# Four more outputs of three norms from x * g, an earlier memory norm, two heads' Gram products in turns, and shared blocks for decay and rate, in a two-block kernel on one core

## The chip, the cores and the metric

The kernel runs on one core of one Trainium2 chip. A core has TensorE (PE, matmuls), VectorE (DVE), ScalarE (ACT), GpSimd (POOL) and SyncE (SP), which here issues DMAs, and each engine executes its own instructions in order. The metric is the device time of one execution in microseconds (us); lower is better.

## The reference

Two transformer-like blocks follow each other on 256 positions of width 1024. The first has three branches (window attention, spatial gating, pooling), gated and merged, then attention to a memory, then a squared-ReLU network. The second prepends 16 meta positions (so 272), has an RWKV-7 layer and a stick-breaking attention layer, each with a convolutional gated network. Nearly each part begins with an RMS norm. What the change touches is this:

```python
def rmsnorm(x, g):
    y = xf * lax.rsqrt(jnp.mean(xf * xf, axis=-1, keepdims=True) + EPS)
    return y * g
# first block
h = rmsnorm(x, g_norm[l, 0])
q, k, v, su, sv, pc, gate = split_columns(h @ w_in[l])
ya = window_sink_attention(q, k, v, attn_sinks[l])
...
merged = jnp.sum(gates * proj, axis=2)        # proj: ya, yb, yc times w_branch
mem_n = rmsnorm(mem, g_mem[l])
...
yf = jnp.square(jax.nn.relu(hf @ w_up[l])) @ w_down[l]
# second block, RWKV-7
w_log = -jax.nn.softplus(-(w0 + jnp.tanh(xw @ w1) @ w2)) - 0.5
a = jax.nn.sigmoid(a0 + (xa @ a1) @ a2)
def step(S, inp):
    sa = jnp.einsum('bhij,bhj->bhi', S, a_t)
    S = S * w_t + sa[..., None] * b_t + v_t[..., None] * k_t
    return S, jnp.einsum('bhij,bhj->bhi', S, r_t)
```

The kernel computes the recurrence in chunks of 64 positions; the Gram products are the products of the chunk's keys with its keys and receptances, of which each head (64 wide, so two heads share 128 partitions) has its own.

## The kernel before, in words

Activations lie transposed, with the features on the partitions: a tensor is 8 tiles (`kc`) of 128 features by 256 (or 272, or 258 in the last layer) positions. Weights come as blocks of 128 x 128 in the order in which the program reads them, eight blocks (512 KB) to a DMA on SP; class `Weights` (L118) issues these DMAs ahead. ACT rounds a group to `whi` and DVE (or POOL, in some stages) subtracts to get `wlo`, and a block is then three matmuls in `mm3` (L382): `wh` by `xh` (L388), `wh` by `xl` (L389) and `wl` by `xh` (L390), where `xh`, `xl` are the two halves of the activation. A "whole" group (`W.whole`, L347 for those of the diff) lands straight in a `whi` or `wlo` buffer, is not split, and a block is one full-precision matmul (L385), which the trace records as two.

`dense` (L403) computes one output of 128 features: all `kc` in a row into one bank, then an eviction. Banks of `pd` are the ordinary ones; `sc` banks (pool `pss`) serve small work.

Class `Norm` (L456 on) normalizes. `steps` writes `raw` = x * g (split, or whole in full precision) and sums the squares. `first` (L490) computes the first four outputs from `raw` by `outer` (L515, `kc` in the outer loop, four banks), since these do not need the root mean square; the result is multiplied by rstd on DVE at the eviction (`ev`). Meanwhile `split` makes the normalized operand: DVE `nt` (x * g * rstd), ACT `xh`, DVE `xl`. The second four outputs (`then`) come by `outer` from it, and the remaining ones by `dense`. `then` is given in four places: w_in, w_up (whole first four), the first network's up-projection of the second block (f_up0, 272 positions, whole first four), and that of the last layer (f_up1, 258 positions, split).

In the first block the gate products (24 outputs of w_in) run with side work between them (`together` of attention, gating and pooling, three steps after each product). Then 24 branch products follow, for features 0 to 3 and then 4 to 7, in each group the gating and pooling branch (n = 1, 2) first and the attention branch (n = 0) after; `norm_mem` (L722), the memory's norm, is the side work there.

In the RWKV stage `decay` (L1091 on) has 16 products with one block each, decay and rate in turns (each weight has 64 rows, padded with zero rows to 128), into the two `pd` banks; ACT takes each with a sigmoid into `LA`. Later the recurrence runs as generators under a planner with due times; its dense products fill the gaps, and Tile's scheduler writes the final order of each engine. `gram(b)` makes for each of two pairs of heads `jj` and head `hh` one product `p0` and four products `pm` in two `f` banks, and evacuates them: ACT copies to `B`, DVE masks into `AK` and `RS`. `fmm` is a matmul (its line in the trace is L986, a helper). All ACT, DVE and POOL work has L214, the line of a helper that records it.

Of the kernel before, what the change touches and what calls it, by code (L numbers as in the profile page):

```python
# [18 lines left out]
P = 128  # L19
D = 1024  # L20
KC = 8
# [27 lines left out]
WHOLE = [n // BLK_G for n in (624, 1456)]  # L49
N_BLOCKS = (42 * 8 + 24 * 4 + 64 + 64 + 32 + 32 + 256 + 256) + (256 + 16 + 16 + 32 + 2 * (352 + 176)) + 256  # L50
# [221 lines left out]
def drain(side):  # L272
    for _ in side:
        pass
# [14 lines left out]
def model(ctx: ExitStack, tc: tile.TileContext, a: dict, out: bass.AP, stage=None):  # L289
# [56 lines left out]
    for first in WHOLE:  # L346
        W.whole.update(range(first, first + 4))  # L347
# [108 lines left out]
    class Norm:  # L456
# [33 lines left out]
        def first(self, items, then=(), ahead=None):  # L490
            def rstd():
                self.r = rstd_of(self.sums, self.n)

            assert not self.whole or len(W.order) // BLK_G in WHOLE
            tiles = outer([x[:2] for x in items], self.raw, self.n, 2, ahead, rstd)
            W.hold = []
            nc.stop()
            dst = xpair(self.n) if then else None
            for i, ((_, ft, ev), ps) in enumerate(zip(items, tiles)):
                if then:  # L500
                    self.split(dst, range(4 * i, 4 * i + 4) if i < 2 else ())
                    if i == 0:
                        table["hold"] += casts
                t = ep[0].tile([P, T], F32, tag="ev", name="ev")[:, :self.n]
                vtt(t, ps, self.r, op=ALU.mult)
                ev(ft, t)
            if then:
                for (_, ft, ev), ps in zip(then, outer([x[:2] for x in then], dst, self.n, 1)):
                    ev(ft, ps)
            return dst  # L510
# [31 lines left out]
    with tc.tile_pool(name="b1", bufs=1) as b1, tc.tile_pool(name="b2", bufs=2) as b2:  # L542
# [172 lines left out]
        side = together(attention(), gating(), pooling())  # L715
        interleave(jobs, side, 3)
        drain(side)

        merged = xpair(S)
        memn = xpair(S)  # L720

        def norm_mem():  # L722
            acc = new_acc(S)
            for kc in range(KC):
                sumsq(mem[:, kc, :], acc, kc == 0, S)
            yield
            r = rstd_of([acc], S)
            for kc in range(KC):
                norm_split(lambda kc: mem[:, kc, :], "g_mem", 0, S, r, memn, (kc,))
                yield  # L730

# [15 lines left out]
        side = norm_mem()  # L747
        order = [(n, ft) for fts in (range(NBR), range(NBR, 8)) for ns in ((1, 2), (0,)) for ft in fts for n in ns]
        interleave([dense(f"w_br{n}", ft, 4, (ya, yb, yc)[n], S, ev_merge(n)) for n, ft in order], side)
        drain(side)  # L750
# [125 lines left out]
    with tc.tile_pool(name="f1", bufs=1) as f1:  # L876
# [30 lines left out]
        W.whole.update(range(group, group + 40))  # L907
# [70 lines left out]
    def rwkv():  # L978
# [11 lines left out]
        with tc.tile_pool(name="rp", bufs=1) as rp, ExitStack() as es:  # L990
# [99 lines left out]

            def decay(n):  # L1091
# [5 lines left out]
            lora = iter(range(16))  # L1097
            decay(16)
# [42 lines left out]

            def scp(tag, shape):
                tag = MAP.get(tag, tag)
                return pq.tile(shape, F32, tag=tag, name=tag, bufs=NBANK[tag])
# [68 lines left out]
            def gram(b):  # L1213
# [20 lines left out]
                for jj in range(2):  # L1234
# [9 lines left out]
                    strict, incl = (lambda q, n, i=i: amask[q, 64 * i:64 * i + 64].unsqueeze(1).broadcast_to([q.stop - q.start, n, 64]) for i in range(2))  # L1244
                    for hh in range(2):
                        r, o = half[hh], other[hh]
                        p0, pm = scp("f", [P, 2, 64]), scp("f", [P, 4, 2, 64])
                        fmm(p0, lhsT=bk2(BK, r, 0), rhs=KR[b][r, jj, :, 0:64], start=True, stop=True)
                        for c in range(4):
                            cs = slice(64 * c + 64, 64 * c + 128)  # L1250
                            im = fmm(pm[:, c], lhsT=bk2(BK, r, c + 1), rhs=KR[b][r, jj, :, cs], start=True, stop=True)
                        nc.scalar.copy(B[r, 8 + jj, :], p0[r, 0, :])
                        vtt(AK[o, jj, 0, :], p0[o, 0, :], amask[o, 0:64], op=ALU.mult)
                        vtt(RS[:, jj, 0, hh, :], p0[:, 1, :], amask[:, 64:128], op=ALU.mult)
                        nc.scalar.copy(B[r, 4 * jj:4 * jj + 4, :], pm[r, :, 0, :])
                        vtt(AK[o, jj, 1:5, :], pm[o, :, 0, :], strict(o, 4), op=ALU.mult)
                        vtt(RS[:, jj, 1:5, hh, :], pm[:, :, 1, :], incl(al, 4), op=ALU.mult)
                        yield 1.1, 1.5
# [513 lines left out]
def arrays(i):  # L1772
# [24 lines left out]
    for n in range(3):  # L1797
# [6 lines left out]
        rw_w2=_pad(i["rw_w2_2"][0], rows=P), rw_a2=_pad(i["rw_a2_2"][0], rows=P, at=(64, 0)), rw_g2=_pad(i["rw_g2_2"][0], rows=2 * P),  # L1804
# [35 lines left out]
```

## Time and profile before

| | us |
|---|---|
| median of 3 runs | 1325.83 (1320.94 to 1328.16) |
| the profiled execution | 1322.63 |
| its span in the trace | 1320.9 |
| TensorE busy | 1268.0 (96%) |
| VectorE busy | 894.8 (68%) |
| ScalarE busy | 705.6 (53%) |
| GpSimd busy | 178.5 (14%) |
| mean granted TensorE clock | 0.988 |

The span is from the first to the last instruction of the profiled execution. An engine's busy time divided by the span is its share. The chain that ended last follows the end of the program back from each instruction to what released it, so it tells whose work sets the end; the groups of instructions and waits tell how long one instruction takes and what an engine waited for.

### The profile page before, as it was taken

To read this page: it belongs to the slowest core of one execution; us is meant where nothing else is said; L and a number is where in the kernel's file an instruction comes from. 1 tells how busy PE (TensorE), PEld (TensorE's weight loads), DVE (VectorE), ACT (ScalarE), POOL (GpSimd) and SP (SyncE) were. 2 spreads that over 40 slices of the span, in tenths; PEclk is the share of its full clock that TensorE was granted. 3 is DMA by queue.
4 is the path that set the end of the run, shared out by engine and by line. 5 is a ranking of instruction groups with operands and counts; after the bars stand their busy time and mean duration, and the time that the engine had idled before them with its cause. 6 is when DMAs were issued, how large, how long until landed. Compare 5 with 4: busy or idle time off the path is not lost.

```text
span 1320.9 us, 25715 instructions
## 1 busy us (share of the span) xinstructions
PE 1268.0 (96%) x10188; PEld 1176.1 (89%) x10188; DVE 894.8 (68%) x1812; ACT 705.6 (53%) x1349; POOL 178.5 (14%) x237
## 2 busy tenths in 40 slices
PE   5999998999999989999999999999999999899997
PEld 5999998888999976877877679999999989899997
DVE  6576586857664457567486468786567557989954
ACT  6566555675554434433242256665457666666643
POOL 1000000000000000434211002553000000135500
PEclk9999999998999999999999989999999999999999
DMA  7554455433555653432202125555554333655663
GB/s 257 157 175 134 155 149 162 153 128 128 178 190 179 188 192 120 128 96 65 71 13 64 50 65 166 170 176 178 175 170 142 125 95 87 191 171 178 191 182 106
DMA packets 54984, 188.16 MB, mean 142 GB/s; under 512 B 7598, under 2 KB 9792, under 8 KB 54736
## 3 DMA queue, kind: packets, MB, share of 16 engines
q1 hardware_dynamic: 53856, 185.27, 44.6%
q8 instruction: 80, 1.31, 0.4%
q0 software_dynamic: 464, 0.73, 0.3%
q10 hardware_dynamic: 544, 0.52, 0.1%
q14 instruction: 40, 0.33, 0.1%
HBM read 185.56 MB, written 1.05 MB: 141 GB/s over the span
## 4 chain that ended last, share of the span: by engine, by line
PE 84%; DVE 10%; ACT 3%; DMA 1%; issue 1%; POOL 1%; SPq 0%; DVEq 0%; ACTq 0%; POOLq 0%
PE pd L388 19%; PE pd L390 19%; PE pd L389 19%; PE pd L385 9%; PE l L986 3%; PE f L986 2%; DVE wlo L214 2%; PE sc L389 1%; PE sc L390 1%; PE sc L385 1%; DVE sh L214 1%; PE sc L388 1%; PE s L986 1%; DVE nt L214 1%; PE sc L1608 1%
## 5 line engine op out<-in xcount | busy, mean ns | idle before, releaser
L214 DVE TENSOR_TENSOR wlo<-raw,whi 128x1024 fp32r<-128x1024 f32 x270 | 332.5, 1233 | 208.6 <-ACT whi L214 204.1
L214 ACT CAST whi<-raw 128x1024 fp32r<-128x1024 f32 x298 | 312.2, 1049 | 299.4 <-PE pd L389 201.4
L388 PE MATMUL pd<-xh,whi 128*128 128x256 f32 (+2 forms) x1264 | 364.0, 289 | 18.9 <-ACT xh L214 12.4
L389 PE MATMUL pd<-xl,whi 128*128 128x256 f32 (+2 forms) x1264 | 361.2, 286 | 6.3 <-DVE xl L214 6.3
L390 PE MATMUL pd<-xh,wlo 128*128 128x256 f32 (+2 forms) x1264 | 361.0, 287 | 0.7 <-DVE wlo L214 0.6
L388 PEld LDWEIGHTS pd<-xh,whi 128*128 128x128 f32 x1264 | 241.8, 192 | 22.8 <-ACT xh L214 13.8
L389 PEld LDWEIGHTS pd<-xl,whi 128*128 128x128 f32 x1264 | 242.6, 192 | 7.4 <-DVE xl L214 7.2
L390 PEld LDWEIGHTS pd<-xh,wlo 128*128 128x128 f32 x1264 | 242.2, 192 | 1.6 <-DVE wlo L214 1.2
L389 PE MATMUL pd<-gl,whi 128*128 128x272 f32 (+1 forms) x352 | 100.1, 285 | 0.0
L388 PE MATMUL pd<-gh,whi 128*128 128x272 f32 (+1 forms) x352 | 100.0, 285 | 0.0
L390 PE MATMUL pd<-gh,wlo 128*128 128x272 f32 (+1 forms) x352 | 99.9, 284 | 0.0
L214 DVE SCALAR_TENSOR_TENSOR c<-pd,vec,c 128x256 f32<-128x256 f32 (+3 forms) x148 | 72.0, 487 | 13.6 <-ACT c L214 11.9
L214 POOL TENSOR_TENSOR wlo<-raw,whi 128x1024 fp32r<-128x1024 f32 x28 | 67.2, 2401 | 77.4 <-ACT whi L214 77.4
L390 PE MATMUL pd<-uh,wlo 128*128 128x256 f32 x256 | 72.5, 283 | 0.4 <-DVE wlo L214 0.4
L388 PE MATMUL pd<-uh,whi 128*128 128x256 f32 x256 | 72.6, 284 | 0.0
L389 PE MATMUL pd<-ul,whi 128*128 128x256 f32 x256 | 72.4, 283 | 0.0
L214 POOL TENSOR_TENSOR s<-s,c 128x272 f32<-128x272 f32 (+1 forms) x44 | 41.9, 953 | 191.3 <-ACT s L214 191.3
L390 PEld LDWEIGHTS pd<-gh,wlo 128*128 128x128 f32 x352 | 66.3, 188 | 0.0
L389 PEld LDWEIGHTS pd<-gl,whi 128*128 128x128 f32 x352 | 66.3, 188 | 0.0
L388 PEld LDWEIGHTS pd<-gh,whi 128*128 128x128 f32 x352 | 66.2, 188 | 0.0
L214 POOL MEMSET hn<- 128x8 f32 x1 | 0.1, 147 | 479.5 <-PE sc L436 479.5
L214 DVE TENSOR_TENSOR gl<-c,gh 128x272 fp32r<-128x272 f32 (+1 forms) x44 | 56.4, 1284 | 1.1 <-ACT gh L214 1.1
(443 smaller groups left out, 2650.8 us busy)
## 6 DMA issues: line engine op xcount, KB each, us to landing
raw<-in_wblk SPq DMA_DIRECT2D x298, 512.0 KB, 3.6
whi<-in_wblk SPq DMA_DIRECT2D x24, 512.0 KB, 3.5
wlo<-in_wblk SPq DMA_DIRECT2D x24, 512.0 KB, 3.6
mem<-in_memT SPq DMA_DIRECT2D x1, 1024.0 KB, 6.7
h<-in_xT SPq DMA_DIRECT2D x4, 128.0 KB, 5.5
h<-in_xT POOLq DMA_DIRECT2D x4, 128.0 KB, 6.5
out<-h SPq DMA_DIRECT2D x2, 256.0 KB, 2.4
out<-h ACTq DMA_DIRECT2D x2, 256.0 KB, 2.5
```

Of the source, the lines that this page charges most:

```text
L214: ins = f(*args, **kw)
L385: first = mm(ps, lhsT=wh, rhs=xh, start=start, stop=stop)
L388: first = mm(ps, lhsT=wh, rhs=xh, start=start, stop=False)
L389: mm(ps, lhsT=wh, rhs=xl, start=False, stop=False)
L390: W.used(mm(ps, lhsT=wl, rhs=xh, start=False, stop=stop))
L986: latest[:] = [nc.tensor.matmul(*args, **kw)]
L1608: mm(z[hh][:, c0:c0 + n], lhsT=k[j][r, s0:s0 + 128], rhs=q[j][r, q0 - Q0:], start=False, stop=True, skip_group_check=True)
```

## The change

1. `first` computes the second four outputs by `dense` from `raw`, the operand of the first four, and multiplies each by rstd at its eviction. The outputs 5 and 8 go to `pd` banks, 6 and 7 to `sc` banks. The normalized operand is still made, for output nine and on. In w_up and f_up0 the second four's weights become whole: the two places have eight whole groups each instead of four.
2. `norm_mem` becomes side work of the gate products, after gating; the branch products have none.
3. In `gram` the `p0` of both heads come first, are evacuated, and then the `pm` of both heads are issued in turns and evacuated.
4. The weights of decay and rate share a block (upper 64 rows the one, lower 64 the other), so 8 blocks instead of 16. Each product uses half the rows, one into a `pd` bank, the other into an `f` bank.

```diff
-WHOLE = [n // BLK_G for n in (624, 1456)]
-N_BLOCKS = (...) + (256 + 16 + 16 + 32 + 2 * (352 + 176)) + 256
+WHOLE = [n // BLK_G for n in (624, 1448)]
+N_BLOCKS = (...) + (256 + 16 + 8 + 32 + 2 * (352 + 176)) + 256
...
-        W.whole.update(range(first, first + 4))
+        W.whole.update(range(first, first + 8))
...
+            def scaled(ft, ev, ps):
+                t = ep[0].tile([P, T], F32, tag="ev", name="ev")[:, :self.n]
+                vtt(t, ps, self.r, op=ALU.mult)
+                ev(ft, t)
...
-            if then:
-                for (_, ft, ev), ps in zip(then, outer([x[:2] for x in then], dst, self.n, 1)):
-                    ev(ft, ps)
+                scaled(ft, ev, ps)
+            old = bank["dense"]
+            for i, (name, ft, ev) in enumerate(then):
+                if i in (1, 2):
+                    bank["dense"] = lambda: pss.tile([P, 512], F32, tag="sc", name="sc")
+                dense(name, ft, KC, self.raw, self.n, lambda ft, ps: scaled(ft, ev, ps))()
+                bank["dense"] = old
...
-        side = together(attention(), gating(), pooling())
+        side = together(attention(), both(gating(), norm_mem()), pooling())
...
-        side = norm_mem()
-        interleave([dense(f"w_br{n}", ft, 4, (ya, yb, yc)[n], S, ev_merge(n)) for n, ft in order], side)
-        drain(side)
+        for n, ft in order:
+            dense(f"w_br{n}", ft, 4, (ya, yb, yc)[n], S, ev_merge(n))()
...
             def decay(n):
                 for _ in range(n):
-                    j, i = divmod(next(lora), 2)
-                    nm, bias = (("rw_w2", "w0"), ("rw_a2", "a0"))[i]
-                    dense(nm, j, 1, hwa, T, lambda ft, ps: act(LA[:, ft, i, :], ps, AF.Sigmoid, bias=vcol(bias, ft)))()
-            decay(16)
+                    j = next(lora)
+                    w = W.blocks([("rw_wa2", 0, j)])[0]
+                    for i, (r, ps) in enumerate(zip(half, (bank["dense"]()[:, :T], scp("f", [P, T])))):
+                        ins = mm(ps, lhsT=w[r, :], rhs=t[r], start=True, stop=True)
+                        act(LA[:, j, i, :], ps, AF.Sigmoid, bias=vcol(("w0", "a0")[i], j))
+                    W.used(ins)
+            decay(8)
...
+                    p0 = [scp("f", [P, 2, 64]) for _ in half]
+                    for hh, r in enumerate(half):
+                        fmm(p0[hh], lhsT=bk2(BK, r, 0), rhs=KR[b][r, jj, :, 0:64], start=True, stop=True)
                     for hh in range(2):
...
-                        p0, pm = scp("f", [P, 2, 64]), scp("f", [P, 4, 2, 64])
-                        fmm(p0, lhsT=bk2(BK, r, 0), rhs=KR[b][r, jj, :, 0:64], start=True, stop=True)
-                        for c in range(4):
-                            im = fmm(pm[:, c], lhsT=bk2(BK, r, c + 1), rhs=KR[b][r, jj, :, cs], start=True, stop=True)
...
-                        yield 1.1, 1.5
+                    yield 0.3, 1.0
+                    pm = [scp("f", [P, 4, 2, 64]) for _ in half]
+                    for c in range(4):
+                        for hh, r in enumerate(half):
+                            im = fmm(pm[hh][:, c], lhsT=bk2(BK, r, c + 1), rhs=KR[b][r, jj, :, cs], start=True, stop=True)
...
+                    yield 0.9, 2.0
```

How the order of the instructions changes, at the places of which the prediction speaks, follows from the compiled programs. The first is PE after the first four outputs of w_in (`xh_120`, `xl_121` are the halves of x * g, `xh_311`, `xl_312` those of the normalized operand). Before:

```order
L388 MATMUL sc_145<-xh_120,whi_257 128x256
L389 MATMUL sc_145<-xl_121,whi_257 128x256
L390 MATMUL sc_145<-xh_120,wlo_258 128x256
L388 MATMUL pd_357<-xh_311,whi_363 128x256
L388 MATMUL sc_358<-xh_311,whi_363 128x256
L388 MATMUL sc_359<-xh_311,whi_363 128x256
L388 MATMUL sc_360<-xh_311,whi_363 128x256
L389 MATMUL pd_357<-xl_312,whi_363 128x256
L390 MATMUL pd_357<-xh_311,wlo_364 128x256
```

Now:

```order
L388 MATMUL sc_145<-xh_120,whi_257 128x256
L389 MATMUL sc_145<-xl_121,whi_257 128x256
L390 MATMUL sc_145<-xh_120,wlo_258 128x256
L388 MATMUL pd_357<-xh_120,whi_360 128x256
L389 MATMUL pd_357<-xl_121,whi_360 128x256
L390 MATMUL pd_357<-xh_120,wlo_361 128x256
L388 MATMUL pd_357<-xh_120,whi_360 128x256
L389 MATMUL pd_357<-xl_121,whi_360 128x256
```

The four outputs no longer stand side by side for each `kc`; one output runs through, from the operand that is already there, and `xh_311` first appears 96 matmuls later.

The second place is PE in the RWKV stage, at the Gram products of the second of eight pairs of heads (L986 before, L993 now, `f<-KR,BK`; L385 are dense products). Before, one head's five and then the other's:

```order
L986 MATMUL f_6141<-KR_5697,BK_6026 128x128
...
L986 MATMUL f_6142<-KR_5697,BK_6026 128x128 x4
L986 MATMUL f_6184<-KR_5697,BK_6026 128x128
L385 MATMUL pd_6101<-xh_5921,wlo_6018 128x272 x7
L385 MATMUL pd_6137<-xh_5921,whi_6040 128x272 x5
L986 MATMUL f_6185<-KR_5697,BK_6026 128x128 x4
```

Now, in that pair, which alone comes out in turns (first part), and in the third, as in the other six (second part):

```order
L993 MATMUL f_6174<-KR_5635,BK_6026 128x128
...
L993 MATMUL f_6175<-KR_5635,BK_6026 128x128
...
L993 MATMUL f_6211<-KR_5635,BK_6026 128x128
L993 MATMUL f_6212<-KR_5635,BK_6026 128x128
L993 MATMUL f_6211<-KR_5635,BK_6026 128x128
L993 MATMUL f_6212<-KR_5635,BK_6026 128x128
...
L993 MATMUL f_6251<-KR_5636,BK_6120 128x128
L993 MATMUL f_6252<-KR_5636,BK_6120 128x128
...
L993 MATMUL f_6297<-KR_5636,BK_6120 128x128 x4
L993 MATMUL f_6298<-KR_5636,BK_6120 128x128 x4
```

The two `p0` stand before all `pm`, both `f` banks go to them together, and the four `pm` of a head still stand together except in the first of these pairs.

The third place is PE at the last attention head in the first block (`sc<-kT,qT` its scores, `sc<-ident,p` its transposes, `sc<-pT,vtok` its output). Before, the scores stand among the products with `ybh`, `ych`, long before the transposes. Now:

```order
L626 MATMUL sc_2014<-kT_136,qT_135 128x128
L626 MATMUL sc_2015<-kT_136,qT_135 128x128
L388 MATMUL pd_2349<-yah_833,whi_2294 128x256
...
L390 MATMUL pd_2366<-yah_833,wlo_2330 128x256
L646 MATMUL sc_2034<-ident_93,p_2027 128x128 x2
L653 MATMUL sc_2039<-pT_2037,vtok_839 64x128 x2
L388 MATMUL pd_2326<-yah_833,whi_2294 128x256
```

Between the scores and the transposes stand 21 matmuls of the first products that read the attention's result.

## Rows read from the trace of the kernel before

**Rows 1.** The page: an engine's busy time and share; the chain's shares by engine.

```profile
PE 1268.0 (96%) x10188; PEld 1176.1 (89%) x10188; DVE 894.8 (68%) x1812; ACT 705.6 (53%) x1349; POOL 178.5 (14%) x237
...
PE 84%; DVE 10%; ACT 3%; DMA 1%; issue 1%; POOL 1%; SPq 0%; DVEq 0%; ACTq 0%; POOLq 0%
```

**Rows 2.** Windows: stretch, length, PE busy (instructions), clock, DMA share, GB/s; w_in, w_up, f_up0.

```profile
25.42:45.20 19.78, 14.40 (x99) 0.83 0.44 134
...
303.40:321.55 18.15, 15.11 (x100) 0.81 0.27 88
781.70:800.20 18.50, 15.36 (x99) 0.82 0.25 81
```

**Rows 3.** Waits of PE by line and releaser: us in total, times, longest.

```profile
PE pd L388 <- ACT xh L214: 12.4, 5, 5.9
```

**Rows 4.** A window inside w_in's second four, same columns as rows 2.

```profile
30.00:37.10 7.10, 5.41 (x25) 0.52 0.22 74
```

**Rows 5.** Timeline of PE: start, length, instruction; a split product, then a whole one.

```profile
219.43 0.28 PE L388 MATMUL pd<-xh,whi 128*128 128x256 f32 x1
...
220.39 0.28 PE L390 MATMUL pd<-xh,wlo 128*128 128x256 f32 x1
...
289.98 1.03 PE L385 MATMUL sc<-xg,whi 128*128 128x256 f32 x4
290.85 1.03 PE L385 MATMUL pd<-xg,whi 128*128 128x256 f32 x4
```

**Rows 6.** Timeline of DVE after rstd in w_in.

```profile
26.84 1.67 DVE L214 SCALAR_TENSOR_TENSOR nt<-h,vec,rstd 128x256 f32<-128x256 f32 x4
28.42 0.75 DVE L214 TENSOR_TENSOR ev<-pd,rstd 128x256 f32<-128x256 f32 x2
...
30.08 1.22 DVE L214 TENSOR_TENSOR wlo<-raw,whi 128x1024 fp32r<-128x1024 f32 x1
31.21 1.09 DVE L214 TENSOR_TENSOR xl<-nt,xh 128x256 fp32r<-128x256 f32 x3
```

**Rows 7.** A window in f_up1's second four, same columns as rows 2.

```profile
1148.90:1152.60 3.70, 0.14 (x2) 1.00 0.44 142
```

**Rows 8.** Branch products: window (PE, PEld, DVE, ACT, POOL busy, clock, DMA), timeline of DVE and PE.

```profile
189.00:208.00 19.00, 15.55 (x121) 14.36 (x120) 18.50 (x44) 10.48 (x22) 0.00 (x0) 1.00 0.40 132
...
190.07 1.67 DVE L214 SCALAR_TENSOR_TENSOR nt<-mem,vec,rstd 128x256 f32<-128x256 f32 x4
...
176.21 0.49 PE L619 MATMUL sc<-kT,qT 64*128 64x128 f32 x4
...
188.49 0.29 DVE L214 TENSOR_TENSOR yal<-sc,yah 128x128 fp32r<-128x128 f32 x1 [1.84 <-ACT yah L214]
```

**Rows 9.** Timeline of PE and ACT at the products of decay and rate (in brackets: idle before).

```profile
523.69 5.10 PE L385 MATMUL pd<-wa,wlo 128*128 128x272 f32 x16
...
527.06 0.95 ACT L214 ACTIVATE LA<-pd,vec 128x272 f32<-128x272 f32 x2 [0.35 <-PE pd L385]
528.36 0.95 ACT L214 ACTIVATE LA<-pd,vec 128x272 f32<-128x272 f32 x2 [0.35 <-PE pd L385]
```

**Rows 10.** Timeline: Gram products, chunk products with halves in turns, a hand-over of an `f` bank.

```profile
557.19 1.16 PE L986 MATMUL f<-KR,BK 64*128 64x128 f32 x10
558.28 0.50 PE L385 MATMUL pd<-xh,wlo 128*128 128x272 f32 x1
...
642.38 0.45 PE L986 MATMUL l<-room 128*64 128x64 f32 x8
642.77 0.45 PE L986 MATMUL l<-KR,S 64*64 64x64 f32 x8
643.05 0.28 PE L986 MATMUL l<-xkh,xkl 64*64 64x64 f32 x4
...
553.37 0.49 PE L986 MATMUL f<-KR,BK 64*128 64x128 f32 x2
...
556.05 0.47 DVE L214 TENSOR_TENSOR room<-f,amask 64x64 f32<-64x64 f32 x2
```

More of the change, by code (lines that the diff above doesn't have):

```diff
@@ L48 @@
 WARM1 = 10
-WHOLE = [n // BLK_G for n in (624, 1456)]
-N_BLOCKS = (42 * 8 + 24 * 4 + 64 + 64 + 32 + 32 + 256 + 256) + (256 + 16 + 16 + 32 + 2 * (352 + 176)) + 256
+WHOLE = [n // BLK_G for n in (624, 1448)]
+N_BLOCKS = (42 * 8 + 24 * 4 + 64 + 64 + 32 + 32 + 256 + 256) + (256 + 16 + 8 + 32 + 2 * (352 + 176)) + 256
 N_DMA = -(-N_BLOCKS // BLK_G)
@@ L503, in first @@
                         table["hold"] += casts
-                t = ep[0].tile([P, T], F32, tag="ev", name="ev")[:, :self.n]
-                vtt(t, ps, self.r, op=ALU.mult)
-                ev(ft, t)
-            if then:
-                for (_, ft, ev), ps in zip(then, outer([x[:2] for x in then], dst, self.n, 1)):
-                    ev(ft, ps)
+                scaled(ft, ev, ps)
[5 more added lines that the diff above has]
+                bank["dense"] = old
             return dst
@@ L714, in model @@
         jobs = [dense("w_in", 18 + i, KC, h0, S, ev_in) for i in range(24)]
-        side = together(attention(), gating(), pooling())
-        interleave(jobs, side, 3)
-        drain(side)
-        merged = xpair(S)
         memn = xpair(S)
@@ L730, in norm_mem @@
                 yield
+        side = together(attention(), both(gating(), norm_mem()), pooling())
+        interleave(jobs, side, 3)
+        drain(side)
+        merged = xpair(S)
         mg = {}
@@ L745, in ev_merge @@
             return ev
-        side = norm_mem()
         order = [(n, ft) for fts in (range(NBR), range(NBR, 8)) for ns in ((1, 2), (0,)) for ft in fts for n in ns]
-        interleave([dense(f"w_br{n}", ft, 4, (ya, yb, yc)[n], S, ev_merge(n)) for n, ft in order], side)
-        drain(side)
+        for n, ft in order:
+            dense(f"w_br{n}", ft, 4, (ya, yb, yc)[n], S, ev_merge(n))()
     def add_post(post, steps, width, stop, pool=(), ready=1, fill=0):
@@ L906, in model @@
         group = len(W.order) // BLK_G + 32
-        W.whole.update(range(group, group + 40))
+        W.whole.update(range(group, group + 39))
         W.first[group] = scale_wa(False)
@@ L1089, in rwkv, with scp @@
             act(t[0:64], t[0:64], AF.Tanh)
+            def scp(tag, shape):
+                tag = MAP.get(tag, tag)
+                return pq.tile(shape, F32, tag=tag, name=tag, bufs=NBANK[tag])
             def decay(n):
                 for _ in range(n):
-                    j, i = divmod(next(lora), 2)
-                    nm, bias = (("rw_w2", "w0"), ("rw_a2", "a0"))[i]
-                    dense(nm, j, 1, hwa, T, lambda ft, ps: act(LA[:, ft, i, :], ps, AF.Sigmoid, bias=vcol(bias, ft)))()
-            lora = iter(range(16))
-            decay(16)
+                    j = next(lora)
[4 more added lines that the diff above has]
+                    W.used(ins)
+            lora = iter(range(8))
+            decay(8)
             base = tc.cur_priority
@@ L1140, in ev_v @@
                 xdone[2] = i0
-            def scp(tag, shape):
-                tag = MAP.get(tag, tag)
-                return pq.tile(shape, F32, tag=tag, name=tag, bufs=NBANK[tag])
             def wt(tag):
@@ L1255, in gram @@
-                        nc.scalar.copy(B[r, 4 * jj:4 * jj + 4, :], pm[r, :, 0, :])
-                        vtt(AK[o, jj, 1:5, :], pm[o, :, 0, :], strict(o, 4), op=ALU.mult)
-                        vtt(RS[:, jj, 1:5, hh, :], pm[:, :, 1, :], incl(al, 4), op=ALU.mult)
-                        yield 1.1, 1.5
+                        nc.scalar.copy(B[r, 8 + jj, :], p0[hh][r, 0, :])
+                        vtt(AK[o, jj, 0, :], p0[hh][o, 0, :], amask[o, 0:64], op=ALU.mult)
+                        vtt(RS[:, jj, 0, hh, :], p0[hh][:, 1, :], amask[:, 64:128], op=ALU.mult)
@@ new lines, in gram @@
+                    yield 0.3, 1.0
+                    pm = [scp("f", [P, 4, 2, 64]) for _ in half]
+                    for c in range(4):
+                        cs = slice(64 * c + 64, 64 * c + 128)
+                        for hh, r in enumerate(half):
+                            im = fmm(pm[hh][:, c], lhsT=bk2(BK, r, c + 1), rhs=KR[b][r, jj, :, cs], start=True, stop=True)
+                    for hh in range(2):
+                        r, o = half[hh], other[hh]
+                        nc.scalar.copy(B[r, 4 * jj:4 * jj + 4, :], pm[hh][r, :, 0, :])
+                        vtt(AK[o, jj, 1:5, :], pm[hh][o, :, 0, :], strict(o, 4), op=ALU.mult)
+                        vtt(RS[:, jj, 1:5, hh, :], pm[hh][:, :, 1, :], incl(al, 4), op=ALU.mult)
@@ L1803, in arrays @@
         rw_wa=np.concatenate([i["rw_w1_2"][0], i["rw_a1_2"][0]], axis=1), rw_g1=_pad(i["rw_g1_2"][0], cols=2 * P),
-        rw_w2=_pad(i["rw_w2_2"][0], rows=P), rw_a2=_pad(i["rw_a2_2"][0], rows=P, at=(64, 0)), rw_g2=_pad(i["rw_g2_2"][0], rows=2 * P),
+        rw_wa2=np.concatenate([i["rw_w2_2"][0], i["rw_a2_2"][0]], axis=0), rw_g2=_pad(i["rw_g2_2"][0], rows=2 * P),
         sb_q=i["sb_wq_2"][0], sb_k=i["sb_wk_2"], sb_v=i["sb_wv_2"], sb_o=i["sb_wo_2"][0],
```

4 lines of the change are left out of this document (removed).

## The prediction

> **What bounds the kernel now.** The page's first part comes first: TensorE is busy 96% of the span, VectorE (DVE) 68%, and the chain that ended last is 84% TensorE and 10% DVE [rows 1]. So a microsecond is gained in two ways only: TensorE gets less work, or one of the holes in its work closes. The holes together are 1320.9 − 1268.0 = 53 us. The reader is to see next where they are: I cut the span into windows at the places that the diff touches. Behind the first four outputs of three norms, the next four outputs take 19.78, 18.15 and 18.50 us, with TensorE busy 14.40, 15.11 and 15.36 of it, at a mean granted clock of 0.81 to 0.83 [rows 2]. The table of waits names what is late there: the high half `xh` of the normalized operand, 12.4 us in five waits, the greatest of the whole table [rows 3]. In the midst of such a place the granted clock is 0.52 for 7 us, the lower of the two levels (1.2 GHz of 2.4) [rows 4]; TensorE had waited before it. So a hole there costs twice, once as a wait and again as slow matmuls after it.
>
> **The sum is made against the profiled execution, 1322.63 us, which is 3.2 below the median of the runs shown, 1325.83. 0.5% of the median, 6.6 us, is about what a measurement of this kernel can tell from no change.**
>
> **Second four outputs.** Now they read x·g, which the first four have just used, and are scaled by rstd at their eviction; nothing in them waits for the normalized operand. Prices: a split block is three matmuls of 0.120 us (from 219.43 to 220.39 are eight) or 0.36; a whole-precision block of 256 columns is 0.4325 (0.87 from 289.98 to 290.85 for four records, two a block) [rows 5]; with 272 columns, by 272/256, 0.46.
> - w_in: 96 × 0.120 = 11.5 in place of 19.78, so 8.3 is there to win. The price lies on DVE: four scalings more. DVE's order after rstd stood before at 26.84 to 32.6 [rows 6]; continued with its starts of 0.40 for an `nt`, 0.34 for an `xl` or `ev`, 1.13 for a `wlo`, in the new order, the last `xl` lands at about 42.5. TensorE reaches the ninth output at 25.42 + 11.5 = 36.9, and has the first halves of three outputs and an attention head's scores, some 6 us, before it needs that one. I leave 0.8 of waiting: **−7.5**, bounds −4 and −8.3.
> - w_up and f_up0: these blocks become whole ones, a larger price on TensorE: 32 × 0.4325 = 13.8 and 32 × 0.46 = 14.7, against 18.15 and 18.50. In exchange four casts and four `wlo` go in each. **−4.0** (a column sum of 0.3 stays in the window) and **−3.8**, bounds −2 for each (another DVE wait of that size) and −4.3, −4.0.
> - f_up1: here TensorE ran ahead of DVE and then stood 3.56 of 3.70 us [rows 7]; DVE sets this stretch. Four scalings of about 0.35 [rows 6] lengthen it: **+1.4**, bounds −1 (the closed hole gives more) and +4 (a low-clock spell more).
>
> **Memory norm.** It moves from the branch products to the gate products. Eight `nt` at 0.40 and eight `xl` at 0.34 to 0.42 are some 6 us of DVE, in a stretch where DVE is busy 18.50 of 19.00 us and TensorE 15.55 [rows 8]; among the gate products TensorE sets the pace. The closed hole is 19.00 − 15.55 = 3.45: **−3.5**, bounds 0 and −5. What is late next is the last attention head: its scores came 12 us ahead of its output (176.21 to 188.49) under other products [rows 8], and now they come inside the first products that read it, with 21 matmuls (2.5 us) to cover them. That hole falls in the stretch in which DVE still catches up, so I cost it at nothing; without that cover it costs some 3.4. Two more ACT table loads lie in ACT's idle half.
>
> **Decay and rate.** Sixteen products into two banks, sixteen sigmoids: ScalarE takes a pair in 0.95 and then waits 0.35 for TensorE, 1.30 a pair [rows 9]. With half-height products into four banks it need not wait: eight pairs × 0.35 = 2.8, and 0.1 for the weight transfer less: **−2.9**, bounds −1 (products of half height run as long, the wait is partly bank release) and −3.7.
>
> **Gram products.** Per pair of heads ten products of 64 rows, 0.218 us each in a row (10 records, five products, in 1.09) [rows 10]. Were all 80 to overlap with the other head's, 80 × 0.218/2 = 8.7 would go. The order shows that they don't: in one pair of eight do the four long products alternate; in the others the four of one head still stand together. What two halves in turns are worth, the nearest row tells: four products of 64 × 64 with halves alternating take 0.28, four of full height 0.39 [rows 10], a ratio of 0.72, thus at most 4.9 for all. I take −1.5 for the one pair and the places where two heads meet. Set against this is the end of the loop: 2.3 us of dense work are left among its last steps where 3.7 stood, and more stands behind it: +1.0. **−0.5** together, bounds −7 and +3.
>
> By the Trainium skill (page "TensorE: Matmul & The Clock Gate", "Part 3: Packing small matmuls — row/col tiling") matmuls on different row groups run concurrently, a weight load overlaps only where the row group differs, and matmuls themselves never change places. By that rule the alternating pair alone would save up to 0.9 and all eight 8.7; the row's 0.72 is a weaker gain for a smaller shape, and no row before shows the 64 × 128 shape in turns.
>
> **Sum:** −7.5 − 4.0 − 3.8 + 1.4 − 3.5 − 2.9 − 0.5 = −20.8, so 1301.8 for an execution like the profiled one, and **1305.0** where the median stands, 3.2 higher.
>
> **The rivals.**
> - *The gap moves to the ninth output* (1314, chance 0.18). The normalized operand is still made by DVE, with more to do: 8 `nt`, 8 `xl`, 8 scalings and 4 `wlo` are 14.5 us from 26.84 on, so 41.3 with nothing else between, and TensorE is there at 38.3. If the other outputs give no cover, 3 us come back in each of three norms, +9. For it: DVE and ACT are what was waited for. Against: in the order the halves of three outputs and the attention stand in between.
> - *Gram turns pay fully* (about 1297, chance 0.08): 8.7 in place of 0.5. Against it is the order.
> - *A slower kernel by banks* (about 1345, chance 0.05). Both `f` banks are now taken by the two short products, then both by the long ones, where before one head's products ran while the other's were evacuated. From a short product's end to its bank being free took up to 2.7 us (553.86 to 556.52) [rows 10]. Sixteen such hand-overs uncovered are +43 against −20.8 elsewhere and turn the result above some 1.7 us each. Against: before, the same evacuations were hidden under the dense products, which still stand between in most pairs.
> - *No change to be told* (about 1321, chance 0.09): the gap moves (+9) and the recurrence, whose plan is made anew, ends 7 us later. For it: the plan shifts all 200 us of that stage. Against: nothing in it got longer.
>
> **How the numbers follow.** My own case has 0.60 and runs from 1294 (the bounds on the good side of w_in, the memory norm and part of the gram) to about 1312. The range 1294 to 1319 takes in the first two rivals; left out are the slower one and most of the no-change one, and tails of mine, in all under 0.2. Faster by over 0.5%: 0.60 + 0.18 + 0.08 = 0.86; within 0.5%: 0.09; slower: 0.05.
>
> **What would show it.** In the profile after: TensorE without a wait from the fifth to the eighth output of w_in, w_up and f_up0, the granted clock there near 1.0, the wait for `xh` of 12.4 us nearly gone; in w_up and f_up0 32 whole blocks in about 14 and 15 us; ScalarE's sigmoids without the 0.35; TensorE at or above 15.55 of 19 in the branch stage; DVE's total down by some 8 `wlo` and up by 16 scalings. The forecast is wrong if a wait for `xl` or `xh` of 3 us or more stands at the ninth output, if waits for `f` banks appear on TensorE in the recurrence, or if the gram products in turns start every 0.11 us.

## The result and the profile after

The change ran in 1301.84 us (median of 4 runs, 1300.16 to 1301.94), against 1323.38 for the kernel before on the same chip (1317.15 to 1328.16): a ratio of 0.9835, 95% interval 0.9806 to 0.9864, 21.5 us. The forecast was 1305.0, range 1294 to 1319, with a sum of −20.8. The profiled execution took 1301.79 us, so it is 20.8 below the one of before. The runs of before that stand beside the experiments fall into two groups, 1319.2 to 1322.8 us at a mean granted clock of 0.988 to 0.992 and 1325.2 to 1327.8 at 0.983 or 0.984, so a median of before can lie in either.

The page of the change: TensorE's busy time fell by 5.7 of the 21.0 us of span ([rows 1] has before's); the rest are holes that closed.

```profile
PE 1262.3 (97%) x10124; PEld 1169.0 (90%) x10124; DVE 893.0 (69%) x1820; ACT 698.8 (54%) x1343; POOL 184.0 (14%) x237
...
PE 85%; DVE 9%; ACT 3%; DMA 1%; issue 1%; POOL 0%; SPq 0%; DVEq 0%; ACTq 0%; POOLq 0%
```

Windows of TensorE over the second four outputs of w_in, w_up (a little over its 32 blocks) and f_up0 (columns as in [rows 2], which are the same places before):

```profile
25.83:37.35 11.52, 11.52 (x98) 1.00 0.48 154
294.40:308.50 14.10, 14.10 (x68) 1.00 0.23 74
761.56:776.02 14.46, 14.46 (x65) 1.00 0.16 46
```

No hole is left in the three, and the granted clock is 1.00 where it was 0.81 to 0.83. 19.78 became 11.52, 18.15 became 14.1, 18.50 became 14.46, for forecasts of 11.5, 13.8 and 14.7. In the table of waits (the first row is before's, beside the one of [rows 3]; the other two are the change's) the normalized operand's high half is down from 12.4 us in five waits:

```profile
PE pd L389 <- DVE xl L214: 6.3, 3, 3.1
...
PE pd L388 <- ACT xh L214: 6.8, 2, 6.0
PE pd L388 <- DVE c L214: 3.8, 2, 3.0
```

The 6.8 that are left have nothing to do with the change: they stand at the start of the program (5.97 and 0.80 us), and so did 5.95 and 1.95 of before's 12.4. At the three places before waited 2.31, 1.97 and 0.25 for `xh`, and more, 3.07 in w_in and 2.90 in f_up0, for the low half `xl`. The last row is new in rank: evictions of the up-projections (`c`), to which the experiments come.

**Where the time went, stage by stage.** The starts of the same matmuls in both PE timelines cut the kernel into stages; each number below is a difference of two such starts, in us (A: the first column sum of w_in to the first branch product. B: to the column sum behind w_out. C: to the last product of w_down. D: to the first Gram product. E: to the last product of rw_o. F: from f_up0's column sum to the first product of its down-projection. G: the same for f_up1). For the full change there are three profiled executions, two of them from repeats beside other kernels. The columns behind are the experiments.

| | before | change, three times | then only | norm only | decay only | Gram only | change without Gram | turns | side4 | pool0 |
|---|---|---|---|---|---|---|---|---|---|---|
| A w_in, gate products | 135.45 | 128.01, 128.01, 128.02 | 128.93 | 133.46 | 135.74 | 134.45 | 128.01 | 128.01 | 129.37 | 128.02 |
| B branch products, w_out | 70.02 | 68.05, 68.98, 68.97 | 69.98 | 67.96 | 70.00 | 69.99 | 68.96 | 69.01 | 65.27 | 68.08 |
| C memory, w_up, w_down | 254.72 | 249.96, 250.24, 250.09 | 249.87 | 253.16 | 254.32 | 253.73 | 250.06 | 250.08 | 249.95 | 250.21 |
| D to the first Gram product | 69.62 | 66.62, 66.61, 66.62 | 69.62 | 69.61 | 66.61 | 69.61 | 66.62 | 66.60 | 66.60 | 66.61 |
| E recurrence | 216.84 | 213.48, 215.18, 214.88 | 217.75 | 215.61 | 215.90 | 213.83 | 215.87 | 214.87 | 214.01 | 213.49 |
| F f_up0 | 129.53 | 127.23, 127.24, 127.23 | 126.44 | 128.39 | 128.66 | 128.23 | 127.22 | 127.24 | 127.23 | 130.90 |
| G f_up1 | 129.37 | 130.72, 129.95, 130.00 | 128.75 | 129.04 | 129.11 | 130.14 | 129.21 | 129.80 | 130.14 | 133.21 |

The stages between differ by less than 1.3 and have no edit in them; the lead-in ahead of A took 22.1 to 25.1 us, whatever the kernel. Three things are to be seen.

Stages that a kernel shares with before still differ by 1 to 3 us in A, C, E, F and G. In A, C and F the old holes stand there, often with a low clock behind them [rows 4]; where they are gone, A and F of the change repeat within 0.03 and C within 0.3. The hole is not always followed by the low clock: in *Gram only* f_up0 has the same wait of 2.90 for `xl` as in before, but a granted clock of 1.00 throughout, and F is 128.23 in place of 129.53. The change's runs lie within 1.8 us here and those of before within 11, but closed holes do not by themselves give that: the runs of the change without Gram, where A, C and F are closed too, lie within 9.2.

The low clock falls elsewhere too. Stage B with the norm moved and three steps is 68.0 to 68.1 where the clock was 1.00 all through it and 69.0 where it was not. Stage E at a clock of 1.00 takes 215.6 to 216.8 with the old order of the Gram products (before, *norm only*, *decay only*, change without Gram) and 213.5 to 214.0 with the new one (the change's first profile, *side4*, *pool0* and *fup1_old*).

And A and B do not hold the same work in all kernels. Where the norm has moved and three steps are taken after each product, the scores, transposes and output of one attention head, 12 matmuls, come behind the first branch product, so in B and no longer in A, and the norm's column sum, two matmuls, comes into A. Stage A of *then only*, the change and *side4* (columns as in [rows 8], up to POOL):

```profile
23.55:152.47 128.92, 128.25 (x1054) 122.66 (x1053) 89.51 (x165) 82.28 (x162) 0.00 (x0) 1.00 0.50 160
...
23.98:151.99 128.01, 127.35 (x1044) 122.24 (x1043) 91.76 (x169) 87.02 (x166) 0.00 (x0) 1.00 0.51 161
...
22.89:152.25 129.36, 128.70 (x1056) 122.86 (x1055) 94.80 (x181) 87.88 (x174) 0.00 (x0) 1.00 0.52 160
```

Ten matmuls fewer in the change and two more in *side4*; the 12 matmuls are worth 1.35 us and the column sum 0.44. So what the norm's move is worth is read from A and B together: 205.5 in before, 198.9 in *then only*, 196.1 and twice 197.0 in the change, 194.6 in *side4*.

### The profile page after: what moved, and what is told of

It is laid out like the page before. It is cut to its first block, busy times and chain, and to the rows that moved or that the text cites. A ratio compares the mean times of both kernels' runs of the same rounds, so it can differ in the third digit from the quotient of the medians.

```text
span 1299.9 us, 25595 instructions
## 1 busy us (share of the span) xinstructions
PE 1262.3 (97%) x10124; PEld 1169.0 (90%) x10124; DVE 893.0 (69%) x1820; ACT 698.8 (54%) x1343; POOL 184.0 (14%) x237
## 3 DMA queue, kind: packets, MB, share of 16 engines
q8 instruction: 80, 1.31, 0.4%
## 4 chain that ended last, share of the span: by engine, by line
PE 85%; DVE 9%; ACT 3%; DMA 1%; issue 1%; POOL 0%; SPq 0%; DVEq 0%; ACTq 0%; POOLq 0%
PE pd L388 20%; PE pd L390 19%; PE pd L389 19%; PE pd L385 10%; PE l L993 3%; PE sc L385 2%; PE f L993 2%; DVE wlo L214 1%; PE s L993 1%; DVE sh L214 1%; PE p L993 1%; ACT whi L214 1%; PE sc L1625 1%; PE sc L1655 1%; DMA raw<-in_wblk 1%
## 5 line engine op out<-in xcount | busy, mean ns | idle before, releaser
L214 ACT CAST whi<-raw 128x1024 fp32r<-128x1024 f32 x290 | 303.7, 1049 | 297.4 <-PE pd L389 204.3
L214 DVE TENSOR_TENSOR wlo<-raw,whi 128x1024 fp32r<-128x1024 f32 x262 | 320.2, 1223 | 186.2 <-ACT whi L214 185.0
L214 DVE SCALAR_TENSOR_TENSOR c<-pd,vec,c 128x257 f32<-128x257 f32 (+3 forms) x144 | 69.7, 485 | 18.0 <-ACT c L214 16.8
L214 POOL TENSOR_TENSOR s<-s,c 128x272 f32<-128x272 f32 (+1 forms) x44 | 47.1, 1070 | 233.2 <-ACT s L214 233.1
L214 DVE TENSOR_TENSOR gl<-c,gh 128x272 fp32r<-128x272 f32 (+1 forms) x44 | 60.4, 1377 | 0.0
```

The costliest lines, as they stand in the source:

```text
L214: ins = f(*args, **kw)
```

## The experiments

**Each part alone**, put into the kernel before; the code is that of the diff ahead, one part at a time. The second four outputs (*then only*):

```diff
+    W.whole.update(range(first, first + 8))
...
+                dense(name, ft, KC, self.raw, self.n, lambda ft, ps: scaled(ft, ev, ps))()
```

> The kernel before with the first part of the change alone (second four outputs from x * g, more whole weights). If the terms simply add, about -13 us: 7.5 in w_in, 4.5 in w_up, 2 in f_up0, and 1.3 given back in f_up1. If the ninth output takes the gap over when nothing else is changed, about -5. A second question is whether the memory norm, which in the full change runs among the gate products, costs anything there: if it is free, the lead at the first branch product is 7.5 here as in the full change; if it costs, the lead is over 8 here.

Measured: 1307.34 us, 0.986 of before (0.9823 to 0.9897). Stage A 128.93 against 134.45 to 135.74 in the three kernels that have it as before; C 249.87 against 253.2 to 254.7; F 126.44 against 128.2 to 129.5. The part does about what was costed, and no gap moves to the ninth output. On the second question: the lead in A is 6.5, and in the full change 7.4, but the 0.9 more are the head that left A for B (1.35) less the norm's column sum (0.44). The norm's work among the gate products costs that column sum and nothing else that shows.

The memory norm (*norm only*):

```diff
-        side = together(attention(), gating(), pooling())
+        side = together(attention(), both(gating(), norm_mem()), pooling())
```

> The kernel before with the memory norm moved to the gate products and nothing else. The prediction's term: no lead at the first branch product and 3.5 us behind the last one. The trace of the full change suggests 1.9 behind the last one. If the norm costs VectorE time that the gate products lack, the lead at the first branch product is below zero by 0.5 or more. If the late attention head uncovers its hole, the total is near 0.

Measured: 1316.81 us, 0.994 (0.9915 to 0.9966). B is 2.06 shorter, not 3.5; the change itself has 2.0, 1.0 and 1.0. But B has one head more in it here. A and B together are 201.4 against 204.4 to 205.7 in the three kernels that have both as before, so 3.0 to 4.3 are gained, old holes in A included. What the term ran into is told with *side4* below.

Shared blocks (*decay only*):

```diff
-                    dense(nm, j, 1, hwa, T, ...)()
...
+                    for i, (r, ps) in enumerate(zip(half, (bank["dense"]()[:, :T], scp("f", [P, T])))):
+                        ins = mm(ps, lhsT=w[r, :], rhs=t[r], start=True, stop=True)
```

> The kernel before with shared blocks for decay and rate alone. The prediction's term is -2.9 (ScalarE no longer waits 0.35 a pair), the recurrence behind it unchanged. Rival: the changed start of the recurrence makes another order there and the total is off by 2 us or more from -3.

Measured: 1315.87 us, 0.9935 (0.9909 to 0.9961). D is 3.01 shorter here and 3.00 in the full change. ScalarE's timeline in the change, where the 0.35 of waiting in [rows 9] is gone:

```profile
507.56 0.86 ACT L214 ACTIVATE LA<-f,vec 128x272 f32<-128x272 f32 x2
508.50 0.94 ACT L214 ACTIVATE LA<-pd,vec 128x272 f32<-128x272 f32 x2
509.34 0.86 ACT L214 ACTIVATE LA<-f,vec 128x272 f32<-128x272 f32 x2
510.08 0.88 ACT L214 ACTIVATE LA<-pd,vec 128x272 f32<-128x272 f32 x2
```

A pair now starts every 0.74 to 0.94 in place of 1.30.

The Gram products (*Gram only*), and the change without them (*change without Gram*):

```diff
+                    p0 = [scp("f", [P, 2, 64]) for _ in half]
...
+                    pm = [scp("f", [P, 4, 2, 64]) for _ in half]
```

> The kernel before with the new order of the Gram products alone. Theory from the trace of the full change: the gain is on TensorE itself, in that products of two heads stand next to each other (two short ones in the time of one, eight long ones in 1.64 instead of 2 x 1.09), about -3 us. The prediction's term was -0.5. If the stage's gain came from another plan that the shared blocks brought about, this alone gives within 1 us of nothing.

> The full change with the Gram products in their old order. If the Gram products' gain adds to the others, 3 us more than the full change. If the recurrence's plan decides, within 1 us of it.

Measured: 1317.43 us alone, 0.994 (0.9918 to 0.9963). The change without them took 1305.54 (1301.04 to 1310.26) against 1301.62 for the change beside it; its runs scatter so much that the 3.9 is only a direction. Stage E is 213.83 alone and 215.87 without; five executions with the old order have 215.6 to 217.8, eight with the new one (two more than the table shows, without *turns*) 213.5 to 215.4. So the gain is the Gram products' own, some 2.2 us by the means (216.4 and 214.2), or 2.4 at a clock of 1.00 alone, and not the shared blocks'.

The whole times of the four one-part kernels lie 18, 9, 10 and 8 us below the median beside them, 45 together, which is twice the full change. The stages that they edit account for some 23 of it, or 25 with A counted for *norm only*. The median beside them, 1325.51, lies in the upper group of before's runs. Against the lower one, the four of 1319.2 to 1321.2 with a mean of 1320.1, they gain 12.8, 3.3, 4.2 and 2.7, together 23. In which stage the executions of the upper group have their low clock stays open, as none of them was profiled; the stage table, not these whole times, carries the terms.

**How the Gram products gain** is read from PE's timeline of the change (a record is half a full-precision product):

```profile
542.43 1.16 PE L993 MATMUL f<-KR,BK 64*128 64x128 f32 x8
543.51 2.10 PE L385 MATMUL pd<-xh,whi 128*128 128x272 f32 x8
...
559.95 1.16 PE L993 MATMUL f<-KR,BK 64*128 64x128 f32 x16
561.04 0.73 PE L993 MATMUL p<-sq,blk 128*128 128x272 f32 x2
...
640.66 0.49 PE L993 MATMUL f<-KR,BK 64*128 64x128 f32 x4
641.08 0.45 PE L993 MATMUL l<-R,xkl 64*64 64x64 f32 x8
...
642.22 1.71 PE L993 MATMUL f<-KR,BK 64*128 64x128 f32 x16
643.86 0.34 PE L993 MATMUL l<-xkl,XT 128*64 128x64 f32 x4
```

Four long products of one head hold TensorE 1.08 (to the next start). In the one pair that the order has in turns, eight hold it 1.09: the second head's are free. Two short ones of the two heads take 0.42, as one alone does. And four and four standing next to each other take 1.64, not 2 × 1.08: they overlap where they meet. Over the stage these rows add up to some 23 us before and 20.3 in the change. That is about the stage's gain; TensorE's waits in the stage fell as well, from 4.9 us to 3.9.

The trace of before had these prices already:

```profile
563.98 1.16 PE L986 MATMUL f<-KR,BK 64*128 64x128 f32 x8
565.06 0.66 PE L1241 MATMUL f<-ident,BK 128*128 128x128 f32 x4
...
659.36 1.38 PE L986 MATMUL f<-KR,BK 64*128 64x128 f32 x10
660.67 0.45 PE L986 MATMUL l<-R,xkl 64*64 64x64 f32 x8
```

Four products of one head take 1.08, and five in a row without overlap 1.31. The five in 1.09 at 557.19 [rows 10] are four of one head and, by the order shown ahead, the first of the other, whose two records start with two of the others' (557.74 and 557.75, twice 557.96): that one is free.

**Strict turns in all pairs** (*turns*), and the change beside it:

```diff
-                            im = fmm(pm[hh][:, c], ...)
+                            im = after(fmm(pm[hh][:, c], ...), *(() if c == 0 and hh == 0 else (im,)))
```

> The full change with the eight long Gram products of every pair of heads tied into strict turns (head, other head, head, ...), where the scheduler left seven of eight pairs as four and four. If turns let two half-height products run at once, each pair's eight take about 0.9 instead of 1.64 us, about -5 us in all. If standing next to each other is already all there is to win (in turns they took 1.79 to the last end, in fours 1.71), within 1 us of the full change.

> The full change once more, as the comparison for the three kernels beside it: 1301 to 1302.

Measured: 1303.80 us (1302.2 to 1304.0) against 1301.62 (1300.77 to 1302.42). The products did what the first theory says, some 17.4 us in all in place of 20.3. PE's timeline of *turns*, at a new wait (in brackets) and at the last pair; between them DVE's timeline at the wait and a window behind it (columns as in [rows 8]):

```profile
583.02 1.33 PE L993 MATMUL f<-room 64*64 64x64 f32 x20 [2.86 <-DVE xkh L214]
...
582.01 0.86 DVE L214 TENSOR_TENSOR xkh<-f,amask 64x256 f32<-64x256 f32 x2
...
583.02:588.40 5.38, 5.38 (x31) 4.41 (x32) 3.13 (x11) 0.56 (x2) 0.63 (x2) 0.50 0.01 3
...
670.82 1.16 PE L993 MATMUL f<-KR,BK 64*128 64x128 f32 x16
671.91 1.12 PE L993 MATMUL s<-MG 64*64 64x32 f32 x32
```

Yet stage E is 214.87, as in the change (213.48 to 215.18), and a wait of 2.86 for `xkh` stands in it, of a size that the change has nowhere in this stage. The product that waits writes an `f` bank and reads only `room`; `xkh<-f` is DVE's evacuation of the long Gram products, which had ended 1.9 us before DVE came to it. So this is a wait for an `f` bank. It is as long as the work that was saved, 2.9, and behind it TensorE ran 5.4 us at a clock of 0.50. What turns would give without that wait is open. My reading "in turns 1.79 to the last end" in the expectation had the wrong pair: 1.79 belongs to one of four and four.

**f_up1 as before** (*fup1_old*):

```diff
+            if self.n == TQ:
+                for (_, ft, ev), ps in zip(then, outer([x[:2] for x in then], dst, self.n, 1)):
+                    ev(ft, ps)
+                return dst
```

> The full change, but the last layer's up-projection (f_up1) computes its second four outputs from the normalized operand as before. If VectorE sets that stretch, as the prediction has it (+1.4 for four scalings), 1.3 us less than the full change. If the closed hole there is worth more than the scalings, slower than the full change.

Measured: 1302.12 us (1301.02 to 1302.57), the same as the change's 1301.62; its stage G is 132.03. Old and new G overlap: 129.04 to 132.03 with the old code, 128.75 to 130.72 with the new. A low clock lies in most of them: where it was equally long, the old code took 129.0 to 129.4 (three executions) and the new one 129.2 to 130.7 (six, by the means 0.8 more). So a price near the forecast's is suggested for the four scalings, but the ranges touch, and the whole times do not show it.

**What the memory norm's term ran into** is in PE's timeline of the change at the first products that read the attention (in brackets: idle before, and for whom):

```profile
182.39 0.52 PE L646 MATMUL sc<-ident,p 128*128 128x128 f32 x2 [0.57 <-DVE p L214]
183.38 0.44 PE L653 MATMUL sc<-pT,vtok 128*64 128x128 f32 x4 [0.46 <-ACT pT L214]
184.18 0.62 PE L388 MATMUL pd<-yah,whi 128*128 128x256 f32 x3 [0.36 <-ACT yah L214]
```

The waits for `gates` of the old stage are gone, but the last head now waits 1.39 in three places. In the change's second profile a low clock follows these; the same stretch of work in the two, which in the second comes 1.59 earlier (columns as in [rows 2]):

```profile
184.00:192.00 8.00, 7.70 (x61) 1.00 0.31 72
```

```profile
182.41:190.41 8.00, 7.81 (x53) 0.79 0.30 74
```

Fewer products fit into it (53 records for 61), and B is 68.98 in place of 68.05. To close the hole, *side4* takes four steps of side work after each gate product, so that the head's scores come some 66 matmuls and more earlier:

```diff
-        interleave(jobs, side, 3)
+        interleave(jobs, side, 4)
```

> The full change with four steps of side work after each gate product instead of three, so that the last attention head's scores come 66 matmuls and more ahead of its transposes again. If the memory norm's term was given back because that head lost its cover (three waits of 1.4 us together at the first products that read it, in some executions 0.9 more at the low clock), the branch stage ends 1.4 to 2.3 us earlier and the whole is as much faster. If VectorE still sets that stretch, as the prediction costed it, no change: the waits only become waits for gates.

> The full change on the chip of the three kernels beside it, for comparison: 1301 to 1302.

Measured: 1301.67 us (1298.83 to 1303.68) beside 1302.76 (1302.24 to 1304.60) for the change. The waits for `p` and `pT` are gone, B is 65.27, 2.8 to 3.7 less than in the change and 4.7 less than before. A is 1.35 longer, because the head's 12 matmuls stand in A again (windows ahead). A and B together are 1.4 less than in the change's first profile and 2.3 less than in the two with the low clock, as the expectation has it; the medians, 1.1 apart, don't tell the two kernels apart.

**f_up0's short term.** In the change DVE is busy all of the 13.60 us behind the second four, and PE then waits for it (window with PE, PEld, DVE, ACT and POOL busy; then PE's timeline):

```profile
776.00:789.60 13.60, 12.76 (x99) 12.34 (x97) 13.60 (x25) 10.17 (x18) 3.80 (x3) 1.00 0.45 146
```

```profile
789.56 0.36 PE L388 MATMUL pd<-xh,whi 128*128 128x272 f32 x1 [0.76 <-DVE c L214]
```

*pool0* takes every second weight split off DVE here; *side4_pool0* has both edits:

```diff
-                if i == 8:
+                if i == 0:
                     W.pool = 2
```

> The full change, but in both of the second block's up-projections GpSimd takes every second weight split from the ninth output on, not only from the seventeenth. If f_up0's term was short (2.3 for 3.8) because VectorE comes late with the evictions after the second four (a wait of 0.76 for c, and slower starts), f_up0 gains 1 us, and f_up1, where the same kind of wait is 3.0 us, up to 3. If it is not VectorE's load, or GpSimd's split of 2.4 us comes too late for TensorE, no gain or a loss of the same size with waits for wlo.

> Both of the two edits beside it. If they act in separate stages, the sum of their gains: 1297 to 1299.

Measured: 1308.44 us (1307.92 to 1309.20) and 1307.55 (1306.58 to 1308.16), 5 to 6 slower. F is 130.90 and G 133.21, each with some low clock in it. The timeline of *pool0* on POOL, DVE and PE shows why, and with it the same stretch as above, which comes 1.43 later here:

```profile
785.49 2.60 POOL L214 TENSOR_TENSOR wlo<-raw,whi 128x1024 fp32r<-128x1024 f32 x1
...
785.76 2.64 DVE L214 TENSOR_TENSOR gl<-c,gh 128x272 fp32r<-128x272 f32 x1
...
790.12 0.36 PE L388 MATMUL pd<-xh,whi 128*128 128x272 f32 x1 [2.12 <-ACT gh L214]
```

```profile
777.43:791.03 13.60, 10.63 (x81) 10.18 (x80) 13.01 (x24) 7.62 (x15) 5.08 (x4) 1.00 0.23 76
```

While GpSimd splits a group, DVE's `gl`, 0.43 us where GpSimd is idle, takes 2.64 and ends 0.3 after GpSimd. So DVE is nearly as busy as before, 13.01 of 13.60 us, though splits were taken from it, and TensorE is busy for 10.63 instead of 12.76. By the Trainium skill (page "SBUF — State Buffer", "Who interferes with whom") a VectorE instruction with two SBUF inputs and a GpSimd instruction that reads SBUF exclude each other, and the later one waits for all of the other; these two rows agree with it. So DVE comes late with the eviction of `c` in the change, but its cure by less DVE work wasn't reached, and taking the scalings out there wasn't tried.

In *then only* this wait is missing and F is 126.44, 0.79 less, although its code in F is the same. DVE's timelines at that place tell the two apart (the change, then *then only*; the same places of F, 9.38 apart):

```profile
787.80 1.21 DVE L214 TENSOR_TENSOR wlo<-raw,whi 128x1024 fp32r<-128x1024 f32 x1
788.93 0.89 DVE L214 SCALAR_TENSOR_TENSOR c<-pd,vec,c 128x270 f32<-128x270 f32 x2
...
797.17 0.43 DVE L214 TENSOR_TENSOR gl<-c,gh 128x272 fp32r<-128x272 f32 x1
797.52 0.49 DVE L214 SCALAR_TENSOR_TENSOR c<-pd,vec,c 128x270 f32<-128x270 f32 x1
797.93 1.21 DVE L214 TENSOR_TENSOR wlo<-raw,whi 128x1024 fp32r<-128x1024 f32 x1
```

Both have the four scalings behind them. In the change a weight split of 1.21 stands ahead of the eviction that TensorE waits for, in *then only* behind it. So the wait of 0.76 hangs on the order that the scheduler gave DVE there, not on the amount of its work alone.

## Why the prediction was right

The range was met, and the time came out nearly to the microsecond; some of that is luck. By the steps of the sum, each with the measured lengths (stage of before minus that of the change's first profile; ranges where old code scatters):

- *w_in −7.5:* A lost 7.44, but 0.9 of that is work that went to B. Alone the part gives 6.5 against before's profile and 5.5 to 6.8 against the three old A, so the term was some 1.0 too high. The reason held: the window is full (8.26 shorter), and the ninth output's cover was enough; the last `xl` ended at 42.8, for an estimate of 42.5. The waits of 12.4 for `xh` were misread: 7.9 of them stand at the program's start, and the hole was more a wait for `xl`. The rival of the moved gap (1314) did not come. Its working has slips: its DVE work of 14.5 comes to 13.2 by the starts used for w_in, and its 38.3 for TensorE was 36.9 there.
- *w_up −4.0:* C lost 4.76, 2.9 to 4.9 over the old ones. Right.
- *f_up0 −3.8:* the window itself lost 4.04 (18.50 to 14.46), but the stage only 2.30, and 1.0 to 2.3 over the old ones. Of the 2.30, about 1.3 is the low clock that before's profile had there and *Gram only* had not. The step that failed let the closed window count in full and priced no wait behind it: DVE, busy all the time, came late with an eviction of `c`, and 0.76 with slower starts around it came back behind the ninth output. Without that wait, in *then only*, F lost 3.09. That the scalings are its cause isn't shown.
- *f_up1 +1.4:* +1.35 in the first profile, but 0.6 in the two others, and old and new overlap. The direction fits, the size is below what these runs can tell.
- *Memory norm −3.5:* A and B together lost 2.9 against *then only* in the first profile and 1.9 in the two others. The step that failed is "that hole falls in the stretch in which DVE still catches up, so I cost it at nothing": the waits for `gates` went with the norm, and the hole stood bare, 1.39, at times with 0.9 of low clock. *side4* covers the head, and A and B together lose 4.3, more than the term.
- *Decay −2.9:* D lost 3.00. Right, in size and cause.
- *Gram and tail −0.5:* E lost 3.36 in the first profile, some 2.2 by the means. The term was mis-sized: it trusted the 0.72 of a row with a smaller shape, while products of two heads that meet overlap fully when in turns (1.09 for eight) and in part when only adjacent (1.64). The price of 0.218 was read from a row that already held a product of the other head, so "no row before shows the 64 × 128 shape in turns" was wrong too: that product was free there. In the one pair in turns two products start together every 0.22 us after the first, one in 0.11, which the prediction named as a sign against itself. The +1.0 for the tail did not show. By the Trainium skill (page "TensorE: Matmul & The Clock Gate", "Part 3: Packing small matmuls — row/col tiling"), weighed in the prediction, matmuls on different row groups run at once, so that eight in turns should cost about what four do; the trace agrees, 1.09 against 1.08.

That the sum of −20.8 met the profiled execution is luck in its sizes: the terms too high (f_up0 by 1.5, w_in by 1.0, the memory norm by 0.6) and those too low (Gram by 2.9, w_up by 0.8) cancelled. The 3.2 added for the median did not come: the change's median, 1301.84, is its profiled execution's time to 0.1, and the forecast of 1305.0 is too high by as much. The slower rival by banks did not come in the change, where no wait for an `f` bank in the recurrence is longer than 0.3 us; but its mechanism is real, for *turns* has one of 2.86.

## What to carry to other kernels

A norm's scale commutes with the product, so the outputs next in line can run from x * g until the normalized operand is ready, as long as the engine that scales at eviction has room; the closed hole also buys back the low clock that stood behind it in most executions, and with it some of the run-to-run scatter. When an edit moves work across the border of two stages, read their sum: here 1.35 us of one head went from A to B and looked like a gain in the one and a loss in the other. When work moves out of a stretch, ask anew what was covered by the engine's lateness there: the wait that it hid is next. Before a price is taken from a row of merged records, look at which operands share the row. Before work is handed to GpSimd to free VectorE, look at whether VectorE's instructions stretch while GpSimd runs.

## What the runs showed of the hardware

- Full-precision products on the two halves of the rows run at once when issued in turns: eight of 64 x 128 hold TensorE 1.09 us, four of one half 1.08, four and four next to each other 1.64.
- A VectorE `TENSOR_TENSOR` on two SBUF operands took 2.64 us instead of 0.43 while GpSimd's split of 2.60 ran.
- The same wait of 2.90 us of TensorE in f_up0 was followed by a low clock in before (0.82 in the mean of the window in [rows 2]) and by none in *Gram only* (1.00 through all of F), with 1.3 us of difference in F; in B, three waits of 1.39 together were followed by a low clock in some executions (0.79 in the window shown) and by none in others, worth 0.9.
